# A two-layer hybrid transformer trunk: a new order for the first layer's mixing steps, a wider output projection, and decay logits in one pass

## The chip, the cores and the metric

The kernel runs on one core of one Trainium2 chip. The metric is the device time of one execution in microseconds (us). Before the change it is 1700.56 us, the median of three runs (1696.95 to 1703.03).

A core has five engines, each with its own queue of instructions that it takes strictly in the order written there: TensorE (PE; its weight loads are listed as PEld), VectorE (DVE), ScalarE (ACT), GpSimd (POOL) and SyncE (SP). SP, ACT and POOL also issue DMAs, and such an issue stands in that engine's queue like any other instruction.

## The reference

Two layers act on 512 latent tokens and 256 context tokens of width 1024; all is fp32. Cut to what matters:

```python
sh1, sc1, ga1, sh2, sc2, ga2 = modulation(c, w_mod, b_mod)      # silu(c) @ w_mod + b_mod, w_mod 1024 x 6144
u = (rmsnorm(x, g_mix) * (1 + sc1) + sh1) @ w_in                # 1024 columns in, split among three head groups
...
la_f = log_sigmoid(r_f @ wg[0] + bg[0]) / 16                    # GLA decay, rank 16 -> 256, and la_b with wg[1]
o_gl = gla_bidir(q, k, v, la_f, la_b, s_f, s_b)                 # gated linear attention, both directions
ql, kl, vl = attn_qkv(aq, ak, av, g_q, g_k)                     # 8 query heads, 2 key heads of 64, rotary positions
mix = concat([pool_mixer(p), gla_output(o_gl, gg), latent_attention(ql, [kc, kl], [vc, vl])]) @ w_out
x = x + ga1 * mix
x = x + ga2 * (relu((rmsnorm(x, g_mlp) * (1 + sc2) + sh2) @ w_up) ** 2 @ w_down)    # hidden width 4096
```

The first layer does this for both token streams with the same weights; the second updates the latents alone, and its context tokens only serve keys, values and the GLA's starting states.

## The kernel before, in words

**Matmuls.** Tokens are held as six tiles of 128 (four latent, two context). Every fp32 operand of a large product is split into a high and a low part in the fp32r format, and the product is done in three passes: high x high, high x low, low x high (`passes`, `tm_matmul` with tokens on the output's partitions, `fm_matmul` with features there). `wload` brings a piece of a weight matrix (512 KB mostly) with a DMA in SP's queue into a tile `raw`; ACT copies it to `whi`, and DVE subtracts to get `wlo`. The tags raw, hi and lo have 3, 5 and 5 buffers. The tags hi and lo are also used by the tiles `rawm` of the modulation's weights and by the softmax's tiles `p`, and raw also by transposed softmax tiles `pe`.

**Stages of a layer.** Input norm and the projections of k, v and gates (`KK`, `GU`); the mixing stage; the output projection (`op`); the MLP. In layer 0 these are 0 to 64, 64 to 384, 384 to 458 and 458 to 1003 us; in layer 1 mixing is 1058 to 1273, the output projection 1273 to 1332, and the MLP ends at about 1690.

**The mixing stage** is written as four generators, each of which issues a few instructions up to its next `yield`:

- `a`: the remaining input projections (`gate_proj`, `k_proj`, `q_proj`, `p_proj`; L930 on). Outputs are `UK`, `UV`, `Uq` (tiles `tm`, token-major) and the pool projections (`fm`, two of them, feature-major, the last of this thread).
- `g`: the GLA in 29 steps for two pairs of heads. `decay` (L655 on) forms the logits `z` for two directions with a matmul of `wg` on `rT` and makes a tree of cumulated decays from them (POOL's `tree`); then seven levels per pair each grow the scaled keys and queries by a tree level (`KK`, `QQ`, L720, DVE), copy the keys (`kc`, ACT), do 48 small matmuls (`att`, L763) and copy the diagonal blocks (`dg`, L783, DVE); then states and outputs (`kbt`, `inc`, `o`, `ss`, `rg`, `ogl`).
- `t`: attention. `k_stack` (L976 on) transposes the keys (`kT`) and splits them into `kh` and `kl`; `q_stack` (L1073 on) does this for one pair of query heads (`qT`, `qs`). Then scores `sc` (L1020, L1021), the negated row maximum `nmx` on DVE, `p` = exp on ACT, transposes `pT`, copies `pe`, and the product with v (`av`).
- `m`: two rounds of the modulation for the rest of the layer, eight steps each of two loads `rawm` and eight matmul records `pm` (L190), closed by `mod_end`, which adds the bias (`brow`), transposes (`pt`) and writes the gates to DRAM (`gaD`).

A string of letters, `STEPS[l]`, sets the order in which the generators are advanced (L1110 on). A scheduler then takes each instruction in that order as its buffers come free, so one engine's row order can differ a little from the order of the string. Before the change each "t" first runs what is left of `a` and of `m`:

```python
        for ch in STEPS[l]:
            if ch == "t":
                run(at_)
                run(mods)
            next(ths[ch], None)
```

In layer 0's string, 33 "a", 17 "g" and 8 "m" stand ahead of the first "t". 

**The output projection** goes through w_out in four blocks of 256 columns, with two loads each (`wcols(..., 256, 2)`); a pair of tiles shares one PSUM tile of 512 columns. `out_res` multiplies by the gate (DVE, `rtmp`) and adds to X (POOL for the first two blocks, DVE for the last two).

Of the kernel before, what the change touches and what calls it, by code (L numbers as in the profile page):

```python
# [18 lines left out]
NL = 512  # L19
# [5 lines left out]
LEVELS = (1, 2, 4, 8, 16, 32, 64)  # L25
C_GV, C_GG, C_R, C_AQ = 768, 1024, 1280, 1312
GT = 5
STEPS = ("aggaamgmagagaaagaaaamgaaaaamagaaaagaaaaaagmgaaaagamggmggmgtt"
         "mggtttmtttgttgtmgtggtttgtttgttmgtmtgttmgtt",
         "ggggagaggaaagaaggaaaaaagaaaagaaaggaagaaggatatgatttttgaatgttg"  # L30
         "tttgggtttgttggttttgtttgt")


@with_exitstack
def hybrid_kernel(ctx, tc, x, c, cx, c_ctx, w_mod, b_mod, g_mix, w_in, w_pool, s_pool, w_gate, b_gate,
# [16 lines left out]
    def nm(s):  # L52
        uid[0] += 1
        return f"{s}_{uid[0]}"
# [137 lines left out]
        mod_end(l, r, modT, pm)  # L192

    def mod_end(l, r, modT, pm):
        brow = lay.tile([128, 512], F32, tag="brow", name=nm("brow"))
        for j in range(4):
            c0 = r * 2048 + j * 512
            nc.scalar.dma_start(brow[32 * j:32 * j + 32], b_mod[l, c0:c0 + 512].partition_broadcast(32))
        V.tensor_tensor(brow, pm, brow, ALU.add)
        pt = psC("pt")  # L200
        for cc in range(4):
            T.transpose(pt[:, cc * 128:(cc + 1) * 128], brow[:, cc * 128:(cc + 1) * 128], ident)
        V.tensor_copy(modT[:, r], pt.rearrange("p (c j r) -> p j c r", c=4, j=4)[:, :, :, 0:2])
        if r >= 1:
            which = r - 1
            for s in range(2):
                for jj in range(2):
                    row = 32 * (jj + (2 if r == 2 else 0)) + s
                    nc.scalar.dma_start(gaD[l, which, s:s + 1, jj * 512:(jj + 1) * 512], brow[row:row + 1, :])

    def modulation_sums(l, r, modT, streams):

# [125 lines left out]
    def layer_tables(l, ta):  # L338

        L = {}  # L340
        mask = ta.tile([128, 5, 32], I32, name=nm("mask"))
        nc.scalar.dma_start(mask, k_mask)
        rk = ta.tile([128, 2, 4, 64], F32, name=nm("rk"))
        nc.scalar.dma_start(rk, k_rope)
        L["gmixT"], L["gmlpT"] = vec[:, l * NV:l * NV + 8], vec[:, l * NV + 8:l * NV + 16]
        o = l * NV
        L["spoolT"], L["bgT"], L["gglaT"] = vec[:, o + 16:o + 18], vec[:, o + 18:o + 22], vec[:, o + 22:o + 23]
        wg = ta.tile([32, 2, 256], F32, tag="wg", name=nm("wg"))
        G.memset(wg, 0.0)
        for d in range(2):  # L350
            nc.scalar.dma_start(wg[16 * d:16 * d + 16, d, :], w_gate[l, d])
# [35 lines left out]
    def run(g):  # L387
        for _ in g:
            pass
# [24 lines left out]
    for l in range(2):  # L414
# [195 lines left out]
        for t in alltiles:  # L610
# [6 lines left out]
        if l == 0:  # L617
            qk_proj(1, 0)
            qk_proj(1, 1)

        rT = gp.tile([32, NT], F32, tag="gt", name=nm("rT"), bufs=GT)
        ps = psA("rT")
        for t in alltiles:
            T.transpose(ps[0:32, t * 128:(t + 1) * 128], GU[:, t, 256:288], ident)
        A.activation(rT, ps[0:32, 0:NT], AF.Copy)
        if l == 1:
            qk_proj(1, 0)
            qk_proj(1, 1)

        if l == 0:  # L630
            load_params(1)
# [290 lines left out]
        def p_proj(bp_):  # L922
            wk = wcols(W, bp_ * 128, 128, 1)
            ps = psA("fm")
            fm_matmul(ps, wk, hT, KT, True, both)
            m_ = slot("pm")
            A.activation(m_[:, 0:N_], ps[:, 0:N_], AF.Copy)
# [45 lines left out]


        kst = []
        def k_stack():  # L976
            ps = psA("kT")
            for t in alltiles:
                T.transpose(ps[:, t * 128:(t + 1) * 128], UKt[0][:, t * 128:(t + 1) * 128], ident)
            for kv in range(2):  # L980
                kh, kl = slot("kh", F32R), slot("kl", F32R)
                src = ps[64 * kv:64 * kv + 64, 0:NT]
                A.activation(kh[0:64], src, AF.Copy)
                sub_lo(kl[0:64], src, kh[0:64])
                A.activation(kh[64:128], src, AF.Copy)
                G.tensor_copy(kl[64:128], kl[0:64].bitcast(F32))
                kst.append((kh, kl))


        nunits = 0  # L990
# [78 lines left out]
        def q_stack(hp):  # L1069
            mix_new(4 + hp)  # L1070
            pq = [psB("qT"), psB("qT")] if both else [psB("qT")]
            for t in live:
                T.transpose(pq[t // 4][:, (t % 4) * 128:(t % 4 + 1) * 128], qview(t, hp), ident)  # L1073
            for hh in range(2):
                qs = slot("qs", F32R)
                for i, pq_ in enumerate(pq):
                    n0, n1 = (0, NL) if i == 0 else (NL, NT)
# [3 lines left out]
                qst[hp * 2 + hh] = qs  # L1081
# [51 lines left out]
        def out_proj(cb, wk, p2, ps):  # L1133
            for i in range(2):
                tm_matmul(ps[:, i * 256:(i + 1) * 256], 2 * p2 + i, wk, mixT, KT)

        def out_res(cb, p2, ps):
            sl = slice(cb * 256, (cb + 1) * 256)
            tmp = bp.tile([128, 512], F32, tag="rtmp", name=nm("rtmp"), bufs=2)
            t3 = tmp.rearrange("p (t d) -> p t d", t=2)  # L1140
            V.tensor_tensor(t3, ps.rearrange("p (t d) -> p t d", t=2),
                            ga[0 if p2 < 2 else 1][:, sl].unsqueeze(1).to_broadcast([128, 2, 256]), ALU.mult)
            (V if cb >= 2 else G).tensor_tensor(XP[p2][:, :, sl], XP[p2][:, :, sl], t3, ALU.add)

        np_ = len(live) // 2
        for cb in range(2):
            wk = wcols(w_out[l], cb * 256, 256, 2)
            pa_ = [psA("op"), psA("op")] if cb % 2 else None
            for p2 in range(np_):
                ps = pa_[p2 // 2][:, (p2 % 2) * 512:(p2 % 2) * 512 + 512] if cb % 2 else psB("op")  # L1150
                out_proj(cb, wk, p2, ps)
                out_res(cb, p2, ps)
        h2 = new_hT("h2")
        msc, msh = [scT[:, 1, s] for s in range(2)], [shT[:, 1, s] for s in range(2)]
        wk = [wcols(w_out[l], cb * 256, 256, 2) for cb in (2, 3)]
# [166 lines left out]
```

## Time and profile before

| | |
|---|---|
| median of three runs | 1700.56 us |
| profiled execution, its own time | 1700.61 us |
| its span | 1698.8 us |
| granted TensorE clock, mean | 0.98 |
| PE busy | 1618.9 us (95%) |
| DVE busy | 911.1 us (54%) |
| ACT busy | 639.1 us (38%) |
| POOL busy | 408.3 us (24%) |
| DMA | 163.36 MB, 96 GB/s over the span |

Busy time of PE is the time with a matmul in the array; its ends are modelled, so overlapping records of consecutive matmuls are longer than the distance between their starts. The clock column of the rows is the share of full speed that TensorE was granted. "x<-y" names the output and inputs of an instruction by the program's tiles, L and a number is the line of the kernel before.

### The profile page before, as it was taken

To read this page: it belongs to the slowest core of one execution; us is meant where nothing else is said; L and a number is where in the kernel's file an instruction comes from. 1 tells how busy PE (TensorE), PEld (TensorE's weight loads), DVE (VectorE), ACT (ScalarE), POOL (GpSimd) and SP (SyncE) were. 2 spreads that over 40 slices of the span, in tenths; PEclk is the share of its full clock that TensorE was granted. 3 is DMA by queue.
4 is the path that set the end of the run, shared out by engine and by line. 5 is a ranking of instruction groups with operands and counts; after the bars stand their busy time and mean duration, and the time that the engine had idled before them with its cause. 6 is when DMAs were issued, how large, how long until landed. Compare 5 with 4: busy or idle time off the path is not lost.

```text
span 1698.8 us, 28409 instructions
## 1 busy us (share of the span) xinstructions
PE 1618.9 (95%) x11899; PEld 1334.4 (79%) x11899; DVE 911.1 (54%) x1302; ACT 639.1 (38%) x1092; POOL 408.3 (24%) x468
## 2 busy tenths in 40 slices
PE   7999968899999999999999999997899999999997
PEld 4989636669978888888888888885669888888885
DVE  4437367753583546546555564486753545545454
ACT  5444246662442312213122234454662522222222
POOL 1111031202201231220311362242111212222225
PEclk9999989999999999999999999997999999999999
DMA  9422530204331313325334232100024223333321
GB/s 320 125 87 65 204 107 3 101 13 127 98 122 53 124 54 121 130 63 186 119 98 161 87 104 81 55 2 1 2 98 126 86 76 99 99 100 99 100 99 50
DMA packets 140255, 163.36 MB, mean 96 GB/s; under 512 B 9412, under 2 KB 116304, under 8 KB 140128
## 3 DMA queue, kind: packets, MB, share of 16 engines
q1 hardware_dynamic: 133312, 147.10, 27.2%
q10 hardware_dynamic: 6816, 14.46, 2.4%
q8 instruction: 93, 1.52, 0.4%
q14 instruction: 34, 0.28, 0.1%
HBM read 157.31 MB, written 4.23 MB: 95 GB/s over the span
## 4 chain that ended last, share of the span: by engine, by line
PE 88%; DVE 4%; ACT 3%; DMA 2%; issue 2%; POOL 1%; SPq 0%; POOLq 0%; DVEq 0%; ACTq 0%
PE dn L335 25%; PE up L316 19%; PE tm L335 8%; PE op L335 7%; PE up L318 5%; PE fm L316 4%; PE av L1047 3%; PE pT L1038 3%; PE up L325 2%; PE fm L318 2%; PE sc L1020 1%; DMA rawm<-in_w_mod_dram 1%; PE att L763 1%; PE pm L190 1%; PE sc L1021 1%
## 5 line engine op out<-in xcount | busy, mean ns | idle before, releaser
L159 ACT ACTIVATE whi<-raw 128x1024 fp32r<-128x1024 f32 (+2 forms) x182 | 184.9, 1031 | 581.2 <-PE dn L335 294.5
L1177 POOL TENSOR_TENSOR X<-X,rtmp 128x512 f32<-128x512 f32 x158 | 215.8, 1368 | 653.5 <-DVE rtmp L1176 653.1
L78 DVE TENSOR_TENSOR wlo<-raw,whi 128x1024 fp32r<-128x1024 f32 (+2 forms) x182 | 224.9, 1245 | 240.2 <-ACT whi L159 237.2
L1176 DVE TENSOR_TENSOR rtmp<-dn,ga 128x512 f32<-128x512 f32 x160 | 109.5, 688 | 215.9 <-PE dn L335 213.0
L335 PE MATMUL dn<-whi,al 128*128 128x512 f32 x480 | 187.2, 390 | 0.0
L335 PE MATMUL dn<-whi,ah 128*128 128x512 f32 x480 | 187.1, 390 | 0.0
L335 PE MATMUL dn<-wlo,ah 128*128 128x512 f32 x480 | 186.3, 390 | 0.0
L316 PE MATMUL up<-h2h,whi 128*128 128x512 f32 x464 | 182.6, 394 | 1.5 <-ACT relu L1219 1.5
L316 PE MATMUL up<-h2h,wlo 128*128 128x512 f32 x464 | 183.2, 395 | 0.0
L316 PE MATMUL up<-h2l,whi 128*128 128x512 f32 x464 | 182.8, 394 | 0.0
L335 PEld LDWEIGHTS dn<-whi,ah 128*128 128x128 f32 x480 | 90.2, 188 | 20.3 <-DVE rtmp L1176 0.8
L316 PEld LDWEIGHTS up<-h2h,whi 128*128 128x128 f32 x464 | 87.1, 188 | 23.5 <-ACT relu L1219 2.5
L335 PEld LDWEIGHTS dn<-whi,al 128*128 128x128 f32 x480 | 90.1, 188 | 19.5
L335 PEld LDWEIGHTS dn<-wlo,ah 128*128 128x128 f32 x480 | 90.1, 188 | 18.9
L316 PEld LDWEIGHTS up<-h2l,whi 128*128 128x128 f32 x464 | 87.1, 188 | 21.8 <-issue 2.5
L335 PE MATMUL tm<-whi,hTh 128*128 128x256 f32 (+1 forms) x352 | 102.3, 291 | 1.1 <-ACT UV L885 1.1
L316 PEld LDWEIGHTS up<-h2h,wlo 128*128 128x128 f32 x464 | 87.2, 188 | 19.6
L335 PE MATMUL tm<-whi,hTl 128*128 128x256 f32 (+1 forms) x352 | 100.8, 287 | 0.0
L335 PE MATMUL dn<-whi,a 128*128 128x512 f32 x320 | 100.0, 395 | 0.4 <-DVE rtmp L1176 0.4
L335 PE MATMUL tm<-wlo,hTh 128*128 128x256 f32 (+1 forms) x352 | 100.0, 287 | 0.0
L335 PE MATMUL op<-whi,mixh 128*128 128x256 f32 x320 | 91.2, 285 | 0.9 <-ACT whi L159 0.9
L335 PE MATMUL op<-wlo,mixh 128*128 128x256 f32 x320 | 90.2, 283 | 0.3 <-DVE wlo L78 0.3
(289 smaller groups left out, 3480.5 us busy)
## 6 DMA issues: line engine op xcount, KB each, us to landing
rawm<-in_w_mod_dram SPq DMA_DIRECT2D x80, 512.0 KB
raw<-in_w_up_dram SPq DMA_DIRECT2D x64, 512.0 KB
raw<-in_w_down_dram SPq DMA_DIRECT2D x64, 512.0 KB
raw<-in_w_in_dram SPq DMA_DIRECT2D x26, 512.0 KB
rawm<-in_w_mod_dram SPq DMA_DIRECT2D x32, 256.0 KB
raw<-in_w_out_dram SPq DMA_DIRECT2D x16, 512.0 KB
raw<-in_w_in_dram SPq DMA_DIRECT2D x12, 256.0 KB
ga<-gaD ACTq DMA_DIRECT2D x6, 512.0 KB
```

Of the source, the lines that this page charges most:

```text
L78: V.tensor_tensor(lo, full, hi.bitcast(F32), ALU.subtract)
L159: A.activation(hi, raw, AF.Copy)
L190: T.matmul(pm[32 * j:32 * j + 32, :], sstat[:, k, :], raw[:, (j % 2) * 512:(j % 2) * 512 + 512], start=(k == 0), stop=(k == KT - 1), skip_ ...
L316: T.matmul(ps[:, 0:NL], a, b[:, 0:NL], start=st, stop=sp_)
L318: T.matmul(ps[:, NL:NT], a, b[:, NL:NT], start=st, stop=sp_)
L325: T.matmul(ps[:, cs], a, b[:, cs], start=(k == 0 and i == 0), stop=(k == nk - 1 and i == 2))
L335: T.matmul(ps, a[:, sl], bb, start=(k == 0 and i == 0), stop=(k == nk - 1 and i == 2))
L763: T.matmul(ps[g * bw:(g + 1) * bw, o0:o0 + bw], a_, b_, start=True, stop=True)
L1038: T.transpose(pt_[:, i * 128:(i + 1) * 128], p_[:, ki * 128:(ki + 1) * 128], ident)
L1047: T.matmul(av_[64 * hh:64 * hh + 64, 0:256], vst, pe[:, hh * 256:hh * 256 + 256], start=(ki == 0), stop=(ki == len(kts) - 1))
L1176: V.tensor_tensor(tmp, ps, ga[0 if t < 4 else 1][:, sl], ALU.mult)
L1177: (V if b == NB - 1 and not both and t == 3 else G).tensor_tensor(X[t][:, sl], X[t][:, sl], tmp, ALU.add)
```

## The change

1. **Order of layer 0's mixing steps.** The new string has 35 "a", 20 "g" and 17 "m" ahead of the first "t", so all modulation steps stand among the projections, and pair 1's decay and first GLA levels too. The run of `mods` at "t" is gone. `qk_proj(1, ...)` becomes the first two steps of `a`; layer 1's string gets "aa" in front and is otherwise the same.
2. **Bias tile of the modulation.** `brow` takes a buffer of the tag raw; its bias loads move from ACT's queue to SP's, and the gate writes `gaD` from ACT's queue to POOL's.
3. **Decay logits.** `wg` becomes an fp32r tile of 96 rows (high, high, low) and `rT` one of 96 rows (high, low, high), so that one pass over 96 rows forms all three products; before, it is an fp32 matmul over 32 rows.
4. **Stacks.** `k_stack` is cut into transposes and one step per key head; the first step of attention does the transposes, the first key head and the first query pair.
5. **Output projection** in two blocks of 512 columns with four loads each; each tile has its own 512 columns of PSUM, and the residual is 128x512 per tile. POOL adds the first block, DVE the second.

```diff
-STEPS = ("aggaamgmagagaaagaaaamgaaaaamagaaaagaaaaaagmgaaaagamggmggmgtt"
+STEPS = ("agamagamgaamgaagmaagmagamagamagamagagamagamagamagamgaamgaagmaagmagamagamttgtgttg"
...
-        brow = lay.tile([128, 512], F32, tag="brow", name=nm("brow"))
+        brow = wp.tile([128, 1024], F32, tag="raw", name=nm("brow"), bufs=3)[:, 0:512]
...
-            nc.scalar.dma_start(brow[32 * j:32 * j + 32], b_mod[l, c0:c0 + 512].partition_broadcast(32))
+            nc.sync.dma_start(brow[32 * j:32 * j + 32], b_mod[l, c0:c0 + 512].partition_broadcast(32))
...
-                    nc.scalar.dma_start(gaD[l, which, s:s + 1, jj * 512:(jj + 1) * 512], brow[row:row + 1, :])
+                    nc.gpsimd.dma_start(gaD[l, which, s:s + 1, jj * 512:(jj + 1) * 512], brow[row:row + 1, :])
...
+        wg = ta.tile([96, 2, 256], F32R, tag="wg", name=nm("wg"))
+        A.activation(wg[0:32], wgf, AF.Copy)
+        A.activation(wg[32:64], wgf, AF.Copy)
+        V.tensor_tensor(wg[64:96], wgf, wg[0:32].bitcast(F32), ALU.subtract)
...
-        rT = gp.tile([32, NT], F32, tag="gt", name=nm("rT"), bufs=GT)
+        rT = gp.tile([96, NT], F32R, tag="gt", name=nm("rT"), bufs=GT)
...
-        A.activation(rT, ps[0:32, 0:NT], AF.Copy)
+        A.activation(rT[0:32], ps[0:32, 0:NT], AF.Copy)
+        sub_lo(rT[32:64], ps[0:32, 0:NT], rT[0:32])
+        A.activation(rT[64:96], ps[0:32, 0:NT], AF.Copy)
...
         def a_thread():
+            for qk in range(2):
+                qk_proj(1, qk)
+                yield
...
         def att_thread():
-            k_stack()
+            k_transposes()
+            k_stack(0)
+            q_stack(0)
             yield
-            q_stack(0)
+            k_stack(1)
             yield
...
             if ch == "t":
                 run(at_)
-                run(mods)
...
+        wk = wcols(w_out[l], 0, 512, 4)
+        for t in live:
+            ps = psB("op")
+            tm_matmul(ps, t, wk, mixT, KT)
+            out_res(t, 0, ps)
...
+        wk = wcols(w_out[l], 512, 512, 4)
         for p2 in range(np_):
             ps = psA("op")
-            for cb in (2, 3):
-                out_proj(cb, wk[cb - 2], p2, ps[:, (cb - 2) * 512:(cb - 1) * 512])
-                if p2 and cb == 2:
+            for i in range(2):
+                tm_matmul(ps[:, i * 512:(i + 1) * 512], 2 * p2 + i, wk, mixT, KT)
+                if p2 and i == 0:
                     norm_pair(p2 - 1, X, h2, msc, msh, psB)
-            for cb in (2, 3):
-                out_res(cb, p2, ps[:, (cb - 2) * 512:(cb - 1) * 512])
+                out_res(2 * p2 + i, 1, ps[:, i * 512:(i + 1) * 512])
```

VectorE's queue in layer 0, just ahead of the first score of attention. Before, it reads (KK and tree are pair 1's; kl and qs are the stacks that the first scores read):

```order
L720 TENSOR_TENSOR KK_965<-KK_965,tree_2429 128x192x2
L720 TENSOR_TENSOR KK_965<-KK_965,tree_2456 128x192x2
L78 TENSOR_TENSOR kl_2670<-kT_2662,kh_2669 64x768
L720 TENSOR_TENSOR KK_965<-KK_965,tree_2429 128x96x4
L720 TENSOR_TENSOR KK_965<-KK_965,tree_2456 128x96x4
L78 TENSOR_TENSOR kl_2676<-kT_2662,kh_2675 64x768
L720 TENSOR_TENSOR KK_965<-KK_965,tree_2429 128x48x8
L720 TENSOR_TENSOR KK_965<-KK_965,tree_2456 128x48x8
L78 TENSOR_TENSOR qs_2691<-qT_2683,qs_2691 64x512
L78 TENSOR_TENSOR qs_2691<-qT_2684,qs_2691 64x256
```

The same place in the queue after the change:

```order
L721 TENSOR_TENSOR KK_992<-KK_992,tree_2232 128x24x16
L721 TENSOR_TENSOR KK_992<-KK_992,tree_2285 128x24x16
L721 TENSOR_TENSOR QQ_2452<-QQ_2452,tree_2232 128x192x2
L721 TENSOR_TENSOR QQ_2452<-QQ_2452,tree_2285 128x192x2
L784 COPY_PREDICATED dg_2454<-mask_735,att_2747 128x192 x2
L199 TENSOR_TENSOR brow_2812<-pm_2040,brow_2812 128x512
L78 TENSOR_TENSOR kl_2840<-kT_2832,kh_2839 64x768
L78 TENSOR_TENSOR qs_2855<-qT_2847,qs_2855 64x512
L78 TENSOR_TENSOR qs_2855<-qT_2848,qs_2855 64x256
```

The growths of KK (L720, now L721) by the levels 192x2 to 24x16 no longer stand among the stacks but ahead of them; a growth of QQ, a masked copy and the modulation's bias add stand directly before kl.

SyncE's queue at the end of the projections in layer 0. Before, the pieces of w_mod stand in one row of 26 up to the first pieces of w_out; here are its last rows:

```order
L188 DMA rawm_2626<-in_w_mod_dram 128x1024
L188 DMA rawm_2630<-in_w_mod_dram 128x1024
L188 DMA rawm_2634<-in_w_mod_dram 128x1024
L188 DMA rawm_2638<-in_w_mod_dram 128x1024
L152 DMA raw_4411<-in_w_out_dram 128x4x256
L152 DMA raw_4417<-in_w_out_dram 128x4x256
```

After the change the queue reads, at the last pieces of w_in:

```order
L188 DMA rawm_2107<-in_w_mod_dram 128x1024
L188 DMA rawm_2111<-in_w_mod_dram 128x1024
L152 DMA raw_2625<-in_w_in_dram 128x8x128
L188 DMA rawm_2187<-in_w_mod_dram 128x1024
L188 DMA rawm_2191<-in_w_mod_dram 128x1024
L152 DMA raw_2690<-in_w_in_dram 128x8x128
L188 DMA rawm_2266<-in_w_mod_dram 128x1024
L188 DMA rawm_2270<-in_w_mod_dram 128x1024
```

Projection weights (raw) now have modulation weights (rawm) in front of them, and 12 rows of rawm follow the last raw of w_in, with one group of bias loads among them.

TensorE's queue at the start of layer 0's output projection after the change (three sums op are open at once; before, these rows have the same pattern with 128x256):

```order
L335 MATMUL op_4441<-whi_4419,mixh_3463 128x512
L335 MATMUL op_4441<-whi_4419,mixl_3464 128x512
L335 MATMUL op_4469<-whi_4419,mixh_3463 128x512
L335 MATMUL op_4469<-whi_4419,mixl_3464 128x512
L335 MATMUL op_4497<-whi_4419,mixh_3463 128x512
L335 MATMUL op_4497<-whi_4419,mixl_3464 128x512
L335 MATMUL op_4441<-wlo_4420,mixh_3463 128x512
```

The first piece of w_out (whi_4419, wlo_4420) feeds three tiles of tokens ahead of the second.

More of the change, by code (lines that the diff above doesn't have):

```diff
@@ L27 @@
 GT = 5
-STEPS = ("aggaamgmagagaaagaaaamgaaaaamagaaaagaaaaaagmgaaaagamggmggmgtt"
-         "mggtttmtttgttgtmgtggtttgtttgttmgtmtgttmgtt",
-         "ggggagaggaaagaaggaaaaaagaaaagaaaggaagaaggatatgatttttgaatgttg"
-         "tttgggtttgttggttttgtttgt")
+STEPS = ("agamagamgaamgaagmaagmagamagamagamagagamagamagamagamgaamgaagmaagmagamagamttgtgttg"
+         "tgttgtttgttgttttgttttgtt",
+         "aaggggagaggaaagaaggaaaaaagaaaagaaaggaagaaggatatgatttttgaatgt"
+         "tgtttgggtttgttggttttgtttgt")
 @with_exitstack
@@ L347, in layer_tables @@
         L["spoolT"], L["bgT"], L["gglaT"] = vec[:, o + 16:o + 18], vec[:, o + 18:o + 22], vec[:, o + 22:o + 23]
-        wg = ta.tile([32, 2, 256], F32, tag="wg", name=nm("wg"))
-        G.memset(wg, 0.0)
+        wgf = ta.tile([32, 2, 256], F32, tag="wgf", name=nm("wgf"))
+        G.memset(wgf, 0.0)
         for d in range(2):
-            nc.scalar.dma_start(wg[16 * d:16 * d + 16, d, :], w_gate[l, d])
+            nc.scalar.dma_start(wgf[16 * d:16 * d + 16, d, :], w_gate[l, d])
+        wg = ta.tile([96, 2, 256], F32R, tag="wg", name=nm("wg"))
+        A.activation(wg[0:32], wgf, AF.Copy)
+        A.activation(wg[32:64], wgf, AF.Copy)
+        V.tensor_tensor(wg[64:96], wgf, wg[0:32].bitcast(F32), ALU.subtract)
         wpl = lay.tile([128, 2, 128], F32, tag="wpl", name=nm("wpl"))
@@ L616, in hybrid_kernel @@
             A.activation(GU[:, t], ps[:, 0:288], AF.Copy)
-        if l == 0:
-            qk_proj(1, 0)
-            qk_proj(1, 1)
-        rT = gp.tile([32, NT], F32, tag="gt", name=nm("rT"), bufs=GT)
+        rT = gp.tile([96, NT], F32R, tag="gt", name=nm("rT"), bufs=GT)
         ps = psA("rT")
@@ L624, in hybrid_kernel @@
             T.transpose(ps[0:32, t * 128:(t + 1) * 128], GU[:, t, 256:288], ident)
[L625 to L628, printed above, removed]
+        A.activation(rT[0:32], ps[0:32, 0:NT], AF.Copy)
+        sub_lo(rT[32:64], ps[0:32, 0:NT], rT[0:32])
+        A.activation(rT[64:96], ps[0:32, 0:NT], AF.Copy)
         if l == 0:
@@ L975, in hybrid_kernel, with k_transposes @@
         kst = []
-        def k_stack():
+        kT = []
+        def k_transposes():
             ps = psA("kT")
@@ L979, in k_stack @@
                 T.transpose(ps[:, t * 128:(t + 1) * 128], UKt[0][:, t * 128:(t + 1) * 128], ident)
[L980 to L987, printed above, removed]
+            kT.append(ps)
+        def k_stack(kv):
+            kh, kl = slot("kh", F32R), slot("kl", F32R)
+            src = kT[0][64 * kv:64 * kv + 64, 0:NT]
+            A.activation(kh[0:64], src, AF.Copy)
+            sub_lo(kl[0:64], src, kh[0:64])
+            A.activation(kh[64:128], src, AF.Copy)
+            G.tensor_copy(kl[64:128], kl[0:64].bitcast(F32))
+            kst.append((kh, kl))
         nunits = 0
@@ L1074, in q_stack @@
             for hh in range(2):
-                qs = slot("qs", F32R)
-                for i, pq_ in enumerate(pq):
-                    n0, n1 = (0, NL) if i == 0 else (NL, NT)
+                qst[hp * 2 + hh] = slot("qs", F32R)
+            for i, pq_ in enumerate(pq):
+                n0, n1 = (0, NL) if i == 0 else (NL, NT)
+                for hh in range(2):
+                    qs = qst[hp * 2 + hh]
                     src = pq_[64 * hh:64 * hh + 64, 0:n1 - n0]
@@ L1080, in q_stack @@
                     sub_lo(qs[64:128, n0:n1], src, qs[0:64, n0:n1])
-                qst[hp * 2 + hh] = qs
         def att_thread():
-            k_stack()
+            k_transposes()
+            k_stack(0)
+            q_stack(0)
             yield
-            q_stack(0)
+            k_stack(1)
             yield
@@ L1132, in hybrid_kernel, with out_res @@
         ga = [load_ga(l, 0, s) for s in range(2 if both else 1)]
[L1133 to L1138, printed above, removed]
+        def out_res(t, cb, ps):
+            sl = slice(cb * 512, (cb + 1) * 512)
             tmp = bp.tile([128, 512], F32, tag="rtmp", name=nm("rtmp"), bufs=2)
[L1140 to L1143, printed above, removed]
+            V.tensor_tensor(tmp, ps, ga[0 if t < 4 else 1][:, sl], ALU.mult)
+            (V if cb else G).tensor_tensor(X[t][:, sl], X[t][:, sl], tmp, ALU.add)
@@ L1145, in hybrid_kernel @@
         np_ = len(live) // 2
[L1146 to L1152, printed above, removed]
+        wk = wcols(w_out[l], 0, 512, 4)
[3 more added lines that the diff above has]
+            out_res(t, 0, ps)
@@ L1153, in hybrid_kernel @@
         h2 = new_hT("h2")
         msc, msh = [scT[:, 1, s] for s in range(2)], [shT[:, 1, s] for s in range(2)]
-        wk = [wcols(w_out[l], cb * 256, 256, 2) for cb in (2, 3)]
+        wk = wcols(w_out[l], 512, 512, 4)
         for p2 in range(np_):
             ps = psA("op")
-            for cb in (2, 3):
-                out_proj(cb, wk[cb - 2], p2, ps[:, (cb - 2) * 512:(cb - 1) * 512])
-                if p2 and cb == 2:
+            for i in range(2):
+                tm_matmul(ps[:, i * 512:(i + 1) * 512], 2 * p2 + i, wk, mixT, KT)
+                if p2 and i == 0:
```

## The prediction

> **What bounds the kernel now.** I read the page's shares of the chain that ended last first, then the slices, then a table of stretches that covers the parts the change touches, and last the waits there.
>
> ```profile
> PE 88%; DVE 4%; ACT 3%; DMA 2%; issue 2%; POOL 1%; SPq 0%; POOLq 0%; DVEq 0%; ACTq 0%
> ...
> PE   7999968899999999999999999997899999999997
> ...
> PEclk9999989999999999999999999997999999999999
> ```
>
> 88% of the chain is TensorE (PE). Its slices (42.5 us each) fall below 9 in the first, in slices 6 to 8 (212 to 340 us, layer 0's attention) and in slices 28 and 29 (layer 1's). So two things pay: less PE work anywhere, and less idle time in those slices.
>
> ```profile
> 64.00:100.00 36.00, 36.00 (x233) 32.86 (x233) 6.13 (x6) 8.55 (x12) 1.34 (x2) 1.00 0.43 126
> 100.00:173.00 73.00, 73.00 (x1078) 65.74 (x1077) 45.30 (x81) 36.97 (x70) 14.36 (x29) 1.00 0.22 68
> 173.10:203.40 30.30, 26.39 (x268) 19.16 (x266) 9.79 (x20) 6.76 (x18) 2.56 (x6) 0.89 0.52 189
> 203.40:233.60 30.20, 30.11 (x352) 14.58 (x351) 12.30 (x28) 10.76 (x16) 6.71 (x14) 1.00 0.71 237
> 233.60:262.00 28.40, 12.93 (x245) 10.41 (x242) 26.66 (x43) 16.79 (x30) 7.56 (x11) 0.70 0.04 11
> 262.00:300.00 38.00, 34.58 (x656) 24.39 (x654) 25.43 (x52) 24.52 (x62) 7.71 (x14) 0.91 0.01 2
> 300.00:340.00 40.00, 35.82 (x291) 25.06 (x292) 27.99 (x49) 23.94 (x56) 11.11 (x18) 1.00 0.29 107
> ...
> 384.30:457.80 73.50, 73.22 (x611) 73.02 (x612) 31.42 (x43) 22.49 (x35) 19.62 (x21) 1.00 0.33 98
> 1058.00:1154.80 96.80, 94.68 (x1107) 81.36 (x1105) 61.34 (x124) 48.36 (x99) 29.32 (x49) 1.00 0.12 34
> 1154.80:1200.00 45.20, 33.34 (x598) 23.93 (x596) 30.12 (x59) 27.02 (x56) 7.23 (x12) 0.77 0.01 2
> ...
> 1273.30:1331.50 58.20, 55.62 (x458) 52.71 (x458) 25.75 (x32) 20.40 (x28) 11.79 (x12) 1.00 0.41 123
> ```
>
> Columns: stretch, length, busy time (count) of PE, its weight loads, DVE, ACT, POOL, then granted clock, DMA share, GB/s. From 64 to 173 us PE has no idle time at all. It idles 3.9 us in 173 to 203, 15.5 us in 233.6 to 262 (where DVE is busy 26.66 of 28.4), then 3.4 and 4.2. In 384 to 458, the output projection, PE is the only limit.
>
> ```profile
> PE sc L1020 <- DVE qs L78: 11.2, 1, 11.2
> PE pm L190 <- DMA rawm<-in_w_mod_dram: 3.9, 3, 3.5
> ...
> PE sc L1020 <- DVE qs L78: 4.5, 1, 4.5
> PE kT L979 <- ACT pm L927: 2.9, 1, 2.9
> ...
> SPq L188 <- PE tm L335: 36.7, 4, 20.3
> SPq L188 <- PE fm L318: 32.2, 4, 11.1
> ```
>
> What was waited for: us, times, longest. The first two rows are layer 0 (170 to 300 us), the next two layer 1 (1140 to 1275), the last two the SP queue in 60 to 240 us. One wait of 11.2 us, the first score for the last half of a stacked q, is most of the hole. The 3.9 us are modulation matmuls out of weights: the loads of w_mod start late, because their slots are held by weights of the projections.
>
> **The change, part by part.** The sum is made against the profiled execution, 1700.61 us, which is within 0.05 us of the median of the three runs, so it serves for both.
>
> *Output projection by 512 columns.* The same products in half as many matmuls.
>
> ```profile
> 385.54 53.90 PE op L335 x447
> ...
> 532.54 32.66 PE dn L335 x144
> ```
>
> These are pieces of the chain (start, us, what, count). 53.90/447 is 120.6 ns for a matmul of 256 columns, 32.66/144 is 226.8 ns for one of 512. Layer 0: 576 x 0.1206 = 69.5 becomes 288 x 0.2268 = 65.3, layer 1: 384 x 0.1206 = 46.3 becomes 192 x 0.2268 = 43.5. Together **-6.8 us**, all of it on the path by the rows above. The first column half now needs four loads in place of two, but the order lets the first load feed three tiles, 18 matmuls or 4.1 us, so I cost the loads at nothing; what hides them is those three open sums, and without them PE would wait some 2 us per layer. The multiplies and adds of the residual stay 128x512 in the same number.
>
> The Trainium skill ("TensorE: Matmul & The Clock Gate", on the back-to-back issue gap) gives a fixed cost of about 2.5 ns beside N/2.4 ns per matmul. By it the 480 matmuls saved are worth 1.2 us and not 6.8, which would speak against this part. The trace's rows imply some 14 ns of fixed cost, so here they disagree, and I go by the rows.
>
> *Decay logits in one fp32r pass.*
>
> ```profile
> 207.73 1.12 PE L664 MATMUL z<-rT,wg 32*128 32x512 f32 x2
> 208.69 0.59 PE L665 MATMUL z<-rT,wg 32*128 32x256 f32 x2
> 209.21 0.66 PE L202 MATMUL pt<-ident,brow 128*128 128x128 f32 x4
> ...
> L664 PE MATMUL z<-rT,wg x16: 587/640/692, 101.8 to 1134.0; 32*128 32x512 f32 x16
> ...
> L625 ACT ACTIVATE rT<-rT x2: 787/794/801, 90.6 to 1058.8; 32x768 f32<-32x768 f32 x2
> ```
>
> One decay holds PE from 207.73 to 209.21, 1.48 us, with two records for each matmul. As fp32r it takes one 512 and one 256 column pass, 0.227 + 0.120 = 0.35 by the rates above; that the pass uses 96 rows and not 128 I take as no difference. 8 decays x 1.13 = **-9.1 us**. They stand in stretches where PE is busy nearly throughout (73.00 of 73.00, 30.11 of 30.20, 94.68 of 96.80), so all of it counts; the least is half, 4.5, if DVE or ACT become the limit behind them. Against it: three small steps to split wg and two more on rT. rT is copied at 90.6 us and first used at 101.8, so two more steps of some 0.8 us are hidden by the 11 us of PE work between (without it they would cost 1.6). The wg copies, of tiles two thirds the size of rT's, stand ahead of the last normalization copies of layer 0 on ACT: 0 to 1 us, taken as 0.
>
> *Modulation steps spread among the projections.* Before, w_mod is loaded in one row of 26 and used after the projections; now most of it is used among them. In 100 to 173 us the DMA share is 0.22, so the bytes fit there.
>
> ```profile
> 173.14 8.00 DMA rawm<-in_w_mod_dram
> ```
>
> This piece of the chain goes. The stretch gives at most 3.9 us of idle time and 0.11 x 30.3 = 3.3 us of lower clock, 7.2; I take **-7**. The new cost: nine w_mod steps, pair 1's decays and its first three GLA levels now share ACT, DVE and POOL with the projections, every engine takes its instructions in order, SP has the w_mod loads and the two bias loads in front of projection weights, and one of three raw slots goes to the bias tile. Its cover: DVE is 62% busy in 100 to 173 us (45.30 of 73). Bounds: 0, or the share of idle time in 300 to 340 us, where DVE is 70% busy and PE idles 4.2 of 40, over the 73 us: 7.6. I take **+3**, nearer the first, since there are no softmax chains in this stage.
>
> *Start of attention in layer 0.*
>
> ```profile
> 238.97 1.94 DVE L720 TENSOR_TENSOR KK<-KK,tree 128x384 f32<-128x384 f32 x2
> 240.84 0.94 DVE L78 TENSOR_TENSOR kl<-kT,kh 64x768 fp32r<-64x768 f32 x1
> 241.82 1.65 DVE L720 TENSOR_TENSOR KK<-KK,tree 128x384 f32<-128x384 f32 x2
> ...
> 244.39 1.65 DVE L720 TENSOR_TENSOR KK<-KK,tree 128x384 f32<-128x384 f32 x2
> 246.07 1.02 DVE L78 TENSOR_TENSOR qs<-qT,qs 64x512 fp32r<-64x512 f32 x2
> ...
> 231.20 1.16 ACTq L209 DMA_DIRECT2D gaD<-brow  x4
> ```
>
> Between 235.7 and 247 us DVE grows KK for pair 1 ahead of the q and k stacks, and the first score waits. In the new order these growths stand under the pool projections (PE's fm). Between the last fm and the first score DVE has one growth of QQ (1.94, as the row for KK), a masked copy, the bias add, one kl and two pieces of qs, about 5 us, and PE has 4 us of its own there. What is late next: the growth ahead of the next level's matmuls (1 to 2 us), and the POOL half of kl, which now stands behind four gaD writes in POOL's queue. On ACT four such issues took 1.16 us; on POOL no row shows one; 1 to 5 us for the four. So 11.2 us become about 3.5 (-7.7), the other 4.3 us of idle time stay, and PE's 12.93 busy us at a clock of 0.70 lose 3.9 that mostly returns: **-12**. Bounds: -4 if the waits just spread over the next levels, -18 if no hole is left.
>
> The clock row says what the hole costs beside its idle time: 0.70 with 11.2 us of waiting, 0.77 in 1154.8 to 1200 after 4.5 and 2.9, 1.00 in 300 to 340 with 4.2 spread out. The Trainium skill's same page, on the clock gate, has the clock halve after an idle window and return after a similar time of work. The trace agrees; with holes under that window the clock would not fall.
>
> *Stacks in layer 1.*
>
> ```profile
> 1159.76 0.81 ACT kh L983
> ...
> 1160.59 0.96 DVE kl L78
> 1161.57 0.80 ACT kh L985
> ```
>
> ACT makes q's first half before the second kv head's k, so the first score no longer stands behind three steps like these, of which one kh and one kl were in its way for certain: **-2** (0 to -3). Two more projection steps at the head of its order are the same ones, written elsewhere: 0.
>
> Sum: -6.8 - 9.1 - 7 + 3 - 12 - 2 = -33.9, so 1666.7, **1667 us**.
>
> **The rivals.** (a) *Only PE work is saved*: the holes of layer 0 move and don't shrink, because DVE is the real limit from 233 to 340 us (80.1 of 106.4 busy). For it: DVE's total is unchanged. Against: it had 27.7 us free in 100 to 173. Time: 1700.6 - 6.8 - 9.1 - 2 = 1683.
>
> (b) *All holes up to 340 us go*, the 7.6 us of idle time in 262 to 340 too, since DVE enters attention without a backlog, and no new waits come: 1667 - 3 - 6 - 7.6 = 1650 (6 is what -18 adds to -12). Against: the softmax order in the middle of attention is nearly the same.
>
> (c) *Slower: SP's queue starves the projections.* A projection's weight load stands behind a w_mod or bias load that waits for its slot or for POOL's gaD writes; all behind it waits too, and PE is out of weights. The queue rows show single waits of 20.3 us, now covered by what was loaded earlier. With nothing won by the schedule (1683) it is back at 1701 at 18 us of PE wait and slower beyond 23; two waits of 20.3 give 1723. Against: one load of 512 KB feeds six tiles with 72 matmuls of 0.12 us, 8.7 us, and the DMA share is 0.22.
>
> (d) *The output projection gains only the fixed cost*: 1667 + 5.6 = 1672.
>
> **How the numbers follow.** Forecast 0.55 (its own range 1657 to 1677), (a) 0.17, (b) 0.10, (c) 0.14, (d) 0.04. About 0.3% (5 us) can be told from no change. All but (c) are faster: 0.86. Of (c), waits of 13 to 23 us, 0.06, give the same, longer ones, 0.08, slower. The range of 8 in 10 takes in (a) and (b) and leaves (c) out: 1648 to 1690.
>
> **What would show it.** Output projection stretches of about 69 and 55 us; decays of some 0.35 us on PE; no 8 us piece of w_mod in the chain and PE's wait on w_mod under 1 us; the wait of the first score in layer 0 under 4 us and no slice below 8 among 6 to 8; layer 1's 4.5 us wait near 2.5. Wrong would be: PE waits on projection weights in 64 to 220 us, a DVE backlog moved to the first levels, POOL's writes ahead of kl making a new hole, or a 96 row pass slower than 0.35 us.

## The result, and the profile after

The changed kernel takes 1678.07 us (median of four runs, 1675.12 to 1679.38), the kernel before 1698.76 beside it: ratio 0.9871, 95% interval 0.985 to 0.9892. Run again later, beside other kernels, it took 1682.42 us (ratio 0.9904, 0.989 to 0.9918). By these two ratios the change is worth 16 to 22 us, where 34 were forecast. The changed kernel's median moved by 4.4 us from one group of runs to the next, that of the kernel before by 1.3 us at most, so kernels are compared below within their group where they can be.

The profiled execution took 1677.11 us. On its page, the chain by engine, PE's slices and its clock:

```profile
PE 85%; DVE 5%; ACT 4%; issue 2%; POOL 2%; DMA 2%; ACTq 0%; SPq 0%; POOLq 0%; DVEq 0%
...
PE   7999979999999999999999999897999999999997
...
PEclk9999989999999999999999999998999999999998
```

Of the three low slices of layer 0's attention one 7 is left. A table of stretches cut at the new kernel's own stages shows what became of the rest (columns as before):

```profile
98.00:173.00 75.00, 73.29 (x1234) 60.43 (x1233) 48.16 (x94) 37.94 (x76) 17.52 (x30) 1.00 0.52 173
173.00:196.00 23.00, 23.00 (x298) 18.01 (x294) 13.26 (x20) 11.49 (x20) 9.52 (x18) 1.00 0.31 98
196.00:222.50 26.50, 26.42 (x360) 21.14 (x352) 14.18 (x32) 9.45 (x15) 6.12 (x6) 1.00 0.23 79
222.50:229.60 7.10, 4.03 (x122) 3.28 (x118) 6.41 (x16) 4.89 (x9) 2.80 (x5) 1.00 0.02 5
229.60:250.00 20.40, 13.44 (x324) 10.32 (x324) 15.52 (x28) 11.62 (x29) 2.71 (x8) 0.67 0.01 2
250.00:290.00 40.00, 38.09 (x368) 26.65 (x368) 20.72 (x43) 21.30 (x49) 5.56 (x11) 0.96 0.01 1
...
1038.50:1113.30 74.80, 69.80 (x955) 63.79 (x954) 48.51 (x96) 41.39 (x85) 16.24 (x27) 1.00 0.15 41
```

Up to 222.5 us, the projections with the modulation among them, PE idles 1.7 us in 75 and then hardly at all: the w_mod wait is gone. Then 10 us of idle time follow between 222.5 and 250, with the clock at 0.67. And a new hole stands in layer 1's projections (the last row), 5 us of idle time in 74.8 us, where 2.1 in 96.8 were.

```profile
PE sc L1028 <- ACT p L1032: 4.9, 4, 1.5
PE pT L1046 <- ACT p L1032: 2.6, 1, 2.6
PE qT L1081 <- DVE qs L78: 2.3, 1, 2.3
...
PE att L764 <- DVE QQ L767: 3.4, 1, 3.4
...
PE kT L985 <- ACT pm L928: 2.9, 1, 2.9
```

Waits of PE after the change (us, times, longest), three rows of layer 0 (60 to 400 us) and two of layer 1 (1020 to 1290). One wait of 11.2 us became several of at most 2.6 us, most of them on softmax's own steps. The wait on L767 did not exist before; the last row did, with the same 2.9 us.

To place the difference, I take the first and last starts of matmuls on PE by the tile that they write: rT (transposes ahead of the decays), z (decays), sc (scores), av, op, dn. The table gives the length of stages in us, from each kernel's profiled execution, in the order in which the kernels are told of below.

| kernel | L0: first z to first sc | first sc to first av | first z to first op | first op to first dn | L1: rT to last z | last sc to last dn |
|---|---|---|---|---|---|---|
| before | 145.1 | 14.7 | 282.5 | 148.1 | 81.5 | 419.1 |
| changed | 129.8 | 22.1 | 266.7 | 146.5 | 79.8 | 421.0 |
| changed, run again | 129.5 | 22.1 | 266.9 | 146.5 | 82.4 | 419.9 |
| projection alone | 142.6 | 16.2 | 280.7 | 147.0 | 81.5 | 422.3 |
| decay alone | 133.7 | 16.6 | 272.8 | 148.3 | 81.5 | 418.4 |
| order alone | 136.7 | 22.1 | 272.8 | 149.5 | 81.5 | 418.0 |
| strings alone | 134.6 | 21.9 | 271.8 | 149.6 | 81.5 | 419.2 |
| changed, 256 columns | 129.4 | 22.1 | 267.4 | 149.6 | 81.4 | 417.7 |
| changed, mixed projection | 128.9 | 22.2 | 267.8 | 146.9 | 81.4 | 418.1 |
| changed, old stacks | 130.3 | 22.3 | 266.8 | 146.5 | 81.4 | 419.4 |
| changed, 17 GLA steps first | 125.1 | 33.8 | 274.9 | 146.2 | 81.5 | 419.9 |
| changed, old bias queues | 128.8 | 23.0 | 270.1 | 146.1 | 81.5 | 420.4 |
| mixed, pool projections split | 136.0 | 17.0 | 264.8 | 145.7 | 81.3 | 420.1 |
| mixed, layer 1's order | 130.1 | 22.2 | 268.5 | 145.8 | 83.2 | 418.5 |

One kernel's stages vary between two executions by up to 2.6 us (79.8 and 82.4). Most of what the change wins is won ahead of layer 0's output projection, whose first op moved by 17.7 us (384.3 to 366.6), of the 24.0 us that last dn moved (1688.0 to 1664.0). Layer 1's last score moved by 25.9 us (1268.9 to 1243.0), so 1.9 us are given back behind it.

### The profile page after: what moved, and what is told of

The parts are those of the page before. It is cut to its first block, busy times and chain, and to the rows that moved or that the text cites. A ratio compares the mean times of both kernels' runs of the same rounds, so it can differ in the third digit from the quotient of the medians.

```text
span 1675.3 us, 27451 instructions
## 1 busy us (share of the span) xinstructions
PE 1599.7 (95%) x11403; PEld 1301.5 (78%) x11403; DVE 910.4 (54%) x1306; ACT 642.4 (38%) x1098; POOL 414.2 (25%) x484
## 4 chain that ended last, share of the span: by engine, by line
PE 85%; DVE 5%; ACT 4%; issue 2%; POOL 2%; DMA 2%; ACTq 0%; SPq 0%; POOLq 0%; DVEq 0%
PE dn L335 25%; PE up L316 19%; PE tm L335 7%; PE op L335 6%; PE up L318 5%; PE fm L316 4%; PE av L1055 3%; PE pT L1046 3%; PE up L325 2%; PE fm L318 1%; PE sc L1028 1%; PE att L764 1%; PE sc L1029 1%; PE pm L190 1%; DVE nmx L1031 1%
## 5 line engine op out<-in xcount | busy, mean ns | idle before, releaser
L228 DVE SCALAR_TENSOR_TENSOR macc<-rawm,sstat,macc 128x1024 f32<-128x1024 f32 x56 | 75.6, 1370 | 7.9 <-DMA rawm<-in_w_mod_dram 7.4
L1031 DVE TENSOR_REDUCE nmx<-sc 128x1 f32<-128x768 f32 x64 | 60.6, 955 | 28.1 <-PE sc L1029 27.6
```

The costliest lines, as they stand in the source:

```text
L228: V.scalar_tensor_tensor(acc[s], raw, c_, acc[s], ALU.mult, ALU.add)
L1031: V.tensor_reduce(nmx[:, i:i + 1], sv, AX.X, ALU.max, negate=True)
```

## The experiments

**The parts alone.** Each is the kernel before with one part of the diff. They ran in one group, beside the kernel before at 1698.53 us.

*Output projection alone*, the last part of the diff:

```diff
-            wk = wcols(w_out[l], cb * 256, 256, 2)
+        wk = wcols(w_out[l], 0, 512, 4)
...
+        wk = wcols(w_out[l], 512, 512, 4)
```

> The kernel before with the output projection by 512 columns alone. Theory A (the gain of PE work is given back where the MLP starts, since the last pair's norm is no earlier): the projection's own stretches shorten by 3 to 4 us in layer 0 and 2 to 3 in layer 1, the stretch from there to the first down product lengthens by about 2 us in each layer, total -1 to -3 us (about 1697). Theory B (each part is worth its price alone, and the parts only get in each other's way): -6.8 us (about 1692).

Measured: 1701.36 us, ratio 1.0019 (1.0008 to 1.003). It is no gain at all but a loss of 1 to 5 us. The matmuls did get cheaper as forecast: in the changed kernel's chain

```profile
366.59 49.30 PE op L335 x216
```

is 228.2 ns each, against twice 120.6. The rows disagree with the Trainium skill's fixed cost ("TensorE: Matmul & The Clock Gate", on the back-to-back issue gap) here too. The saving is lost around the matmuls and behind them: in layer 1 the last op comes 58.3 us after the last score in both profiles. VectorE's rows around the end of layer 1's projection, before (last op ends at 1327.5) and with the projection alone (at 1326.9), start, length, instruction:

```profile
1319.48 0.76 DVE L280 TENSOR_SCALAR xn<-X,rstd 128x1024 f32<-128x1024 f32 x1 [2.19 <-POOL rstd L253]
1320.95 0.76 DVE L280 TENSOR_SCALAR xn<-X,rstd 128x1024 f32<-128x1024 f32 x1 [0.71 <-POOL rstd L253]
...
1335.31 0.75 DVE L280 TENSOR_SCALAR xn<-X,rstd 128x1024 f32<-128x1024 f32 x1
```

```profile
1319.79 1.29 DVE L1137 TENSOR_TENSOR rtmp<-op,ga 128x512 f32<-128x512 f32 x2 [5.77 <-PE op L335]
...
1323.87 0.75 DVE L280 TENSOR_SCALAR xn<-X,rstd 128x1024 f32<-128x1024 f32 x1 [1.59 <-ACT whi L159]
...
1336.52 0.75 DVE L280 TENSOR_SCALAR xn<-X,rstd 128x1024 f32<-128x1024 f32 x1 [0.26 <-POOL rstd L253]
```

Before, the norm of the first pair's second tile starts 6.5 us ahead of the end of the projection, with the 512 column form 3.0 ahead; the last norm comes 7.8 us after the end before, 9.6 after it now. One candidate for the cause is TensorE's order: in the second half in layer 0, before, come 96 matmuls for the first pair, 96 for the second, 96 for the third; with 512 columns, after a few single rows, 16 for the first pair, 19 for the second, 24 for the first, 21 for the third, 24 for the second, 27 for the third. The weights arrive in four pieces one by one, so sums of several tiles are open at once and finish late together: the first pair is complete after 72 of the half's 144 matmuls, where it was after 96 of 288; in layer 1 after 72 of 96, where it was after 96 of 192.

A second candidate stands beside it, on ScalarE, which splits the MLP's weights and also takes part in the norms. Its rows just behind layer 1's projection, first before, then with the projection alone, and below them a piece of the changed kernel's chain:

```profile
1327.87 1.05 ACT L159 ACTIVATE whi<-raw 128x1024 fp32r<-128x1024 f32 x1
...
1330.20 1.06 ACT L159 ACTIVATE whi<-raw 128x1024 fp32r<-128x1024 f32 x1 [2.39 <-DMA raw<-in_w_up_dram]
```

```profile
1300.21 4.23 DMA raw<-in_w_up_dram
```

With 512 columns ScalarE waits 2.39 us for a piece of w_up, and the squares for the last norms stand behind it in its queue. The load starts late: in the chain it follows a copy on VectorE (wlo) that itself follows an op matmul, which fits four pieces of w_out that stay in use to the end of the half and hold the slots. All six profiles with 512 columns in the second half have this wait there (2.2 to 2.4 us), none of the other eight has it. The MLP's first products need norms and weights, and the time from the last score to the last down product grows from 419.1 to 422.3 us. How much of that is the order of finishing and how much the late load is not shown. This profile also has 2.7 us more in layer 1's attention, which the median of all runs can't separate; that part stays open.

*Decay logits alone*, parts wg and rT of the diff:

```diff
-        rT = gp.tile([32, NT], F32, tag="gt", name=nm("rT"), bufs=GT)
+        rT = gp.tile([96, NT], F32R, tag="gt", name=nm("rT"), bufs=GT)
```

> The kernel before with the decay logits as one fp32r pass alone. Theory A (PE work is saved, but in layer 1 VectorE then becomes late for the next GLA matmuls, a new wait of 3 to 4 us on L766): layer 1 gains 1 to 2 us, layer 0 up to 4.6, total -3 to -6 us. Theory B (all of the priced PE work counts): -9.1 us (about 1690).

Measured: 1689.54 us, ratio 0.9948 (0.9931 to 0.9965), 9 us. A decay now holds TensorE 0.36 us (z from 99.94 to 100.30 us in the changed kernel), where 0.35 were forecast. By size the gain is theory B's, by place neither's, though theory A's wait in layer 1 did come. Layer 1's stretch from rT to the last decay is 81.5 us as before; layer 0's mixing is 9.7 shorter. Waits of PE, two of layer 0 (100 to 300 us) and one of layer 1 (1043 to 1149):

```profile
PE sc L1027 <- DVE qs L78: 9.0, 1, 9.0
...
PE pm L190 <- DMA rawm<-in_w_mod_dram: 1.9, 3, 1.2
```

```profile
PE att L770 <- DVE QQ L773: 3.4, 1, 3.4
```

In layer 1 the saved PE work turns into a wait of 3.4 us for VectorE's first scaling of QQ behind the decay. In layer 0 the 4.5 us of work are saved, and the two big waits shrink besides, 11.2 to 9.0 and 3.9 to 1.9 us; 4.5 + 2.2 + 2.0 = 8.7 of the 9.7.

*Order alone*: strings, bias tile and queues, stacks, without decay and projection.

> The order part alone: new strings, modulation spread, bias tile and its queues, split stacks; without the decay pass and the 512 column projection. Theory A (the order carries most of the gain): -13 to -18 us (about 1684). Theory B (order gives what is left after -6.8 and -9.1 of the others): -5 us (about 1694).

Measured: 1686.24 us, ratio 0.9936 (0.9918 to 0.9953), so 8 to 14 us; the median, -12.3, is just short of theory A's range. *Strings alone*, with bias tile, queues and stacks as before:

```diff
-                run(mods)
```

> Only the strings, the modulation no longer run in one go at the first t, and the two moved projection steps; bias tile, its queues and the stacks as before. Theory A (the string does it, the stacks and queues are side issues): within 3 us of the run with the whole order part, so -11 to -17. Theory C (the first score is early only because of the split stacks, and the bias loads in ACT's queue cost): less than half of the whole order part's gain, -7 or less.

Measured: 1688.61 us, ratio 0.9944 (0.9925 to 0.9962). That is 9.9 us, within 2.4 us of the whole order part. The strings do it; whether the rest of the order part adds anything the runs can't tell.

The three parts alone sum to +2.8 - 9.0 - 12.3 = -18.5 us by medians, about the change's -16 to -22. In layer 0's mixing they don't add: decay and order shorten it by 9.7 each alone, by 15.1 together (the row with 256 columns), 15.8 in the whole change. Both shrink the same wait of the first score, which fits, but no run separates that.

**Beside the other parts.** One group, with the changed kernel at 1682.42 us and the kernel before at 1699.8.

> The changed kernel itself, run beside the others to have its time on the same chip: 1675 to 1680 us, 19 to 23 less than before.

It came at 1682.42 us, 2 us slower than expected; the others are read against this run. *256 columns as before*, the rest changed:

> The changed kernel with the output projection of before (256 columns). Theory A (alone the 512 column form made the kernel 3 us slower, since the norm of a pair of tiles starts later and the MLP with it; the same holds beside the other parts): 1 to 4 us faster than the changed kernel, about 1675. Theory B (the form costs something only in the old order of attention): 3 to 7 us slower than the changed kernel.

Measured: 1679.61 us, ratio to before 0.9894 (0.9876 to 0.9911): 2.8 us faster than the changed kernel by medians, in theory A's range. The intervals overlap, and the changed kernel's first group was at 0.9871, so a gain is not shown; theory B's loss is ruled out against this group alone. *Mixed*: the first half of the projection by 512 columns, the second, ahead of the norm, as before:

```diff
-        wk = wcols(w_out[l], 512, 512, 4)
+        wk = [wcols(w_out[l], cb * 256, 256, 2) for cb in (2, 3)]
```

> The changed kernel with 512 columns in the first half of the output projection alone; the second half, ahead of the norm, in blocks of 256 as before. Theory A (half of the saving on matmuls stays, 3.4 us, and the norm is early again, so the MLP starts as before): 3 to 6 us faster than the changed kernel and 1 to 3 faster than with 256 columns throughout. Rival D (what costs is that the weights of a half of w_out hold four of five slots to its end): no better than the changed kernel.

Measured: 1677.63 us, ratio to before 0.9875 (0.9861 to 0.9889), 4.8 us less than the changed kernel in this group. Its norms (last op ends at 1304.9) are early again:

```profile
1298.33 0.75 DVE L280 TENSOR_SCALAR xn<-X,rstd 128x1024 f32<-128x1024 f32 x1 [0.71 <-POOL rstd L253]
...
1312.67 0.75 DVE L280 TENSOR_SCALAR xn<-X,rstd 128x1024 f32<-128x1024 f32 x1
```

6.6 us ahead of the end and 7.8 behind it, as before the change, and the time from the last score to the last dn is 418.1. This is the fastest version of its group, by an interval that just clears the changed kernel's; against the changed kernel's first group (0.9871) it is no clear gain. It does not decide between theory A and rival D's slots: blocks of 256 also set the slots free sooner, and the wait for w_up is gone here as well.

*Old stacks* (both key heads, then the first query pair) in both layers:

> The changed kernel with the key and query stacks of before (both key heads, then the first query pair). Theory A (the first score needs one key head and one query pair only; what is behind it on VectorE comes later anyway): 1 to 4 us slower than the changed kernel. Theory E (VectorE is the limit there and only the order of its work changes): no difference, within 1 us.

Measured: 1681.11 us, ratio 0.9896 (0.9882 to 0.9911): no difference that the runs can tell, theory E's size. In its table row the stages of layer 0 agree with the changed kernel's within 1 us; the 2 us forecast for layer 1's first score are not there in the end.

**What in the order does it.** One group, the kernel before at 1699.87 us; no changed kernel beside them. *Three GLA steps fewer ahead of the first t:*

```diff
-  ...agaagmaagmagamagamttgtgttg...
+  ...agaagmaamaamaamttgtggggttg...
```

> The changed kernel with three GLA steps fewer ahead of the first t (17 as before the change; pair 1's first levels behind the first scores' steps), all modulation steps still among the projections. Theory A (the wait for the first score went because pair 1's early levels moved under the pool projections): 4 to 9 us slower than the changed kernel, half or more of the order part's 12. Theory M (the gain of the order is the modulation's loads, hidden now; the levels only move): within 2 us of the changed kernel.

Measured: 1686.52 us, ratio 0.9923 (0.991 to 0.9936), 4 to 8 us behind the changed kernel's two medians, theory A's size and not theory M's. But theory A's reason, the wait for the first score, is not what the trace shows. The first score comes earlier than in any other kernel, and it helps nothing:

```profile
L1027 PE MATMUL sc<-kh,qs x28: 277/415/794, 224.7 to 297.6; 128*128 128x512 f32 x14, 128*128 128x256 f32 x14
...
L1054 PE MATMUL av<-pe,UV x60: 379/379/687, 258.5 to 299.6; 128*64 128x256 f32 x60
...
PE att L763 <- DVE QQ L720: 7.9, 2, 4.8
...
224.70:258.50 33.80, 18.89 (x660) 14.84 (x658) 25.33 (x51) 16.68 (x37) 4.02 (x8) 0.62 0.01 3
```

The rows are the first and last starts of sc and av, a wait of PE, and the stretch between. From first score to first av pass 33.8 us, with PE at 56% and the clock at 0.62: GLA's matmuls stand between the scores in TensorE's queue and wait for VectorE (7.9 us), and the scores behind them wait too.

*Old bias queues* (own buffer, ACT's queue):

> The changed kernel with the bias tile in its own buffer, its loads and the gate writes in ACT's queue, as before. Theory Q (four gate writes in POOL's queue hold the second half of kl back by 2 us ahead of the first score, and one raw buffer is missing): 1 to 3 us faster than the changed kernel. Theory A (that wait lies beside VectorE's own backlog): within 1 us.

Measured: 1680.96 us, ratio 0.9889 (0.9874 to 0.9905): between the changed kernel's two ratios, so no difference that can be told. The rows of the changed kernel's POOL show how little was at stake:

```profile
224.13 1.98 POOL L209 DMA_DIRECT2D gaD<-brow  x4 [12.46 <-DVE brow L199]
226.16 0.82 POOL L994 CAST kl<-kl 64x768 fp32r<-64x768 f32 x1
```

The four writes hold POOL for 1.98 us, and kl's second half, whose first half was ready at 225.25, for about 1; it is done at 226.98, and the first score starts only at 229.7.

*Pool projections split*, on the mixed kernel, so that GLA's matmuls can stand between their pieces; the string has 24 GLA steps ahead of the first t in place of 20, four more and not the five expected:

```diff
-            fm_matmul(ps, wk, hT, KT, True, both)
+            for k0 in range(0, KT, 2):
+                fm_matmul(ps, wk, hT, KT, True, both, k0, k0 + 2)
+                if l == 0 and k0 + 2 < KT:
+                    yield
```

> The changed kernel with the mixed output projection (512 columns, then 256) and, in layer 0, the pool projections issued in four pieces each, with five more GLA steps between the pieces, so that all levels of pair 1 but the last two or three stand ahead of the first score. In the changed kernel's trace VectorE idles 8 us under the last pool projection, since the next level's matmuls stand behind it on TensorE. Theory A (VectorE's backlog at the start of attention is what is left of the hole): 5 to 10 us faster than with the mixed projection alone, 10 to 15 faster than the changed kernel. Rival (softmax's own chain of maximum, exponential and transposes sets the pace there): no more than 2 us faster than with the mixed projection alone.

The ground for it is this row of the changed kernel:

```profile
221.67 1.04 DVE L721 TENSOR_TENSOR QQ<-QQ,tree 128x384 f32<-128x384 f32 x2 [8.03 <-PE att L764]
```

Measured: 1678.3 us, ratio 0.9878 (0.9859 to 0.9897), the mixed kernel's ratio. By time the rival holds. From first score to first av it takes 17.0 us and no longer 22.2, but the first score is later (136.0), and the largest wait of PE in 222 to 300 us is

```profile
PE sc L1029 <- ACT kh L994: 7.8, 2, 6.2
```

so by the trace the stacks on ACT now end last there, and not the softmax's chain that the rival named. With 264.8 us the mixing is 2 to 3 us shorter than in the changed and the mixed kernel, which the whole runs don't resolve.

*Layer 1's order*, on the mixed kernel, one projection step moved ahead of the first grown level:

```diff
-         "aaggggagaggaaagaaggaaaaaagaaaagaaaggaagaaggatatgatttttgaatgt"
+         "aaggggaagaggaagaaggaaaaaagaaaagaaaggaagaaggatatgatttttgaatgt"
```

> The mixed kernel (512 columns in the first half of the output projection alone) with one gate projection step of layer 1 moved ahead of the first grown GLA level of pair 0. Theory A (the faster decays gain nothing in layer 1, since TensorE then waits 3.4 us for VectorE's L767 and its clock drops; with 5.5 us more work ahead the wait goes): the stretch from the first transpose of rT to the last decay becomes 2 to 4 us shorter than the 81.5 it is in nearly every kernel so far, about 1674 to 1676. Rival (the levels of pair 0 are a chain through VectorE and ACT, and the wait turns up at the next level): the stretch stays at 81 to 82, no gain.

Measured: 1682.24 us, ratio 0.9914 (0.9891 to 0.9936), no gain over the mixed kernel's 0.9875 in another group. The wait on QQ is gone and others stand in its place (1030 to 1120 us):

```profile
PE tm L335 <- ACT UV L885: 2.2, 1, 2.2
PE kbt L694 <- DVE KK L720: 2.2, 1, 2.2
```

The stretch is 83.2 us, so the rival holds: the wait turned up elsewhere. In all profiles this stage takes 79.8 to 83.2 us, with the decays' 4.5 us of PE work or without. What holds it there was not settled.

## Why the prediction was right or wrong

1678 us came where 1667 were forecast, and 1682 in the second group: inside the range of 8 in 10, just outside the forecast's own 1657 to 1677. The direction was right and the largest waits were the ones named; two terms, the projection and the start of attention, were too large, and the decays' term landed by luck. Rival (a)'s 1683 is near too, but by chance: it keeps the projection's 6.8 us, which did not come, and gives nothing to the schedule, which brought most of the gain. Step by step:

- **Output projection, -6.8: wrong, the sign too.** The price per matmul was right (228.2 ns against 226.8; its rows give 6.9 and not 6.8). Wrong was "all of it on the path": it counted the stage and not what hangs on its end. Two things there were put at nothing, and the runs don't tell them apart. The open sums of several tiles, which the prediction saw only as cover for the loads, make the pairs finish late, so the norm starts late; and the MLP's first weights come late, a wait of 2.2 to 2.4 us, most likely for slots that w_out still holds. Measured alone +1 to +5 us; beside the other parts the loss is likely (2.8 and 4.8 us by medians within one group) but not clear of the changed kernel's own spread. Rival (d), 1.2 us of gain left, came nearer, though for another reason.
- **Decay logits, -9.1: right in size (8.8 by the ratio), wrong in place, so the size is luck.** It said 4.5 in each layer, since PE was busy 94.68 of 96.80 us in layer 1. Taken out there, the work left idle time in its place, the case that the prediction had named for its least, 4.5; layer 0 gave twice its share because waits shrank with it.
- **Modulation spread, -7 and +3: right as far as the rows show; no run has it alone.** The wait on w_mod is no longer among PE's waits, and 100 to 222 us has under 2 us of idle time, less than the 3 allowed for. DMA share in 98 to 173 us went from 0.22 to 0.52. SP's queue starved nobody (rival c).
- **Start of attention, -12: right in mechanism, too large.** The wait of 11.2 us went, and the place of pair 1's early levels is worth 8 us of mixing (17 steps first: 274.9 against 266.7). It isn't worth it through the first score, which came earlier still with 17 steps, but through what follows. From first score to first av the time grew from 14.7 to 22.1 us in the changed kernel, 7.4 us, so a good part was spread over what comes next; the prediction's "1 to 2 us" for that was the mis-sized term, and its bound of -4 was the case "if the waits just spread". Rival (a) is half true.
- **Stacks in layer 1, -2: nothing in the total that the runs can tell.** The 4.5 us wait is gone; the changed kernel with the old stacks agrees with the one beside it within 1.3 us.
- **Sum.** Decay and order were added though both take from layer 0's holes: 20.6 us of layer 0's mixing were forecast for them, 15.8 came; what each gives alone adds up to 19.4. By whole runs the order part alone, with the stacks, gave 12.3 where 18 were forecast.

The clock row kept its place in it: 0.67 in 229.6 to 250 us of the changed kernel, 0.62 in the 33.8 us of the kernel with 17 steps first. The prediction said that with holes under the idle window the clock would not fall. It fell. The longest waits of PE at the start of attention in the changed kernel are these:

```profile
228.41 0.41 PE L1081 MATMUL qT<-ident,Uq 128*128 128x128 f32 x2 [2.29 <-DVE qs L78]
...
246.66 0.89 PE L1046 MATMUL pT<-ident,p 128*128 128x128 f32 x3 [2.65 <-ACT p L1032]
```

The Trainium skill's rule of the same page, on the clock gate, has the clock halved after an idle window of about 3.4 us. No wait here is that long, and yet the granted clock was 0.50 from about 229.7 to 239.8 us and from about 246.8 to 253 us. In layer 1 a wait of 3.4 us (1064.1 to 1067.5) left it at 1.00, and one of the same length in the mixed kernel (up to 1069.3) was followed by 0.66 in 1070 to 1075 us. So single waits don't tell when the clock falls, and a hole that is cut in pieces can still have the price of the low clock. From 226.1 to 229.7 and from 244.0 to 247.9 us, 3.6 and 3.9 us, TensorE did nothing but 0.41 and 0.89 us of transposes; whether these count as work for the clock no run shows.

## What to carry to other kernels

Price a faster stage by what starts at its end: if the next stage needs whole rows of a tile, the order in which tiles finish can be worth more than a cheaper matmul, and so can the slots that its weights hold when the next stage's are due. In a queue that is taken in order, an early first matmul proves nothing; follow the first result that the next chain needs (here av, not sc). Gains that are read from the same hole don't add. And work taken out of a stage that is 97% busy on one engine may still give nothing if another chain there is as long.

## What the runs showed of the hardware

The changed kernel's rows of the decay and of the projection by tile (shortest, median and longest ns, first and last start):

```profile
L665 PE MATMUL z<-rT,wg x8: 397/398/501, 99.9 to 1112.8; 96*128 96x512 f32 x8
```

```profile
L335 PE MATMUL op<-whi,mixl x160: 387/389/398, 366.9 to 1300.7; 128*128 128x512 f32 x160
```

A matmul of 512 columns cost 228.2 ns in the output projection where one of 256 costs 120.6, and a pass over 96 rows costs about what one over 128 does: 398 ns in the record against 389. Four small DMA writes issued by POOL held its queue for 1.98 us, where ACT's queue took 1.16. With the writes back in ACT's queue the time was the same within the runs (1680.96 us).
